# Stage seams of a two-layer decoder trunk: sums of squares on POOL, and weight splits queued behind the transposed input

## The chip, the cores and the metric

The kernel runs on one core of a Trainium2 chip. The metric is the device time of one execution in microseconds. The engines are named as the profile names them: PE (matrix products and transposes; PEld its weight loads), DVE (elementwise), ACT (activations and copies), POOL (a few small operations here), SP (issues loads). Each engine runs its instructions in the order in which they stand in its queue.

## What is computed

Two layers over 256 tokens of width 1024, in float32. Each layer is a SwiGLU FFN, a mixer, a second FFN, and a gated per-layer input embedding (PLE), each added to the running sum h and each behind an RMS norm:

```python
for i in range(DEPTH):
    h = h + 0.5 * swiglu(rmsnorm(h, ffn1_norm[i]), ffn1_wg[i], ffn1_wu[i], ffn1_wd[i])
    h = h + hybrid_mixer(rmsnorm(h, mix_norm[i]), w_in[i], ...)
    h = h + 0.5 * swiglu(rmsnorm(h, ffn2_norm[i]), ffn2_wg[i], ffn2_wu[i], ffn2_wd[i])
    gate = jax.nn.sigmoid(rmsnorm(h, ple_norm[i]) @ ple_w_gate[i])
    h = h + gate * (p[i] @ ple_w_proj[i])
return rmsnorm(h, final_norm)
```

`rmsnorm(h, g)` is `h * rsqrt(mean(h*h) + EPS) * g`, token by token. The mixer holds a gated short convolution and a Mamba-2 branch. The weights (some 270 MB) are read once.

## The kernel before

**Split products.** PE multiplies in a rounded format (fp32r). To keep float32 precision, each operand is split in two: a first part (the rounded value) and a second part (the rest), and three products are added. A weight chunk is loaded by SP in two halves of 128x1024 into `raw` tiles (`fetch`, lines 113 to 119; `NRAW` = 5 buffers). For each half ACT writes the first part `whi` (line 98) and DVE subtracts it from `raw` to get the second part `wlo` (line 96). A `raw` buffer is free, and its next load can be issued, when both have read it. There are seven pairs of `whi` and `wlo`.

**Order of the work.** The program is a list of items (`add`, line 133), each a function with the weight chunks that it reads. `emit` (lines 149 to 191) goes through the list; before each item `refill` splits as many coming halves as there are free pairs. The instructions thus recorded are then set in order for each engine by the compiler's scheduler, so that the queue of an engine can differ a little from the order of the code. `queued(ins)` (lines 106 to 111) orders the instructions of a block behind `ins` on its engine.

**A stage seam.** The tokens are two tiles of 128, tile 0 and tile 1. Between two stages stands a seam (`seam`, lines 353 to 370): the last products of the old stage, tile 0's first, then tile 1's; for each tile `finish` adds the result to h (line 538 for an FFN, line 1042 for the mixer), in two halves; `square` (line 326, ACT) gives for each half a sum of squares `ss`; `prepare` (lines 329 to 335) adds the two sums and EPS to `var` (line 288), takes the power -1/2 on POOL as `rstd` (line 294), and writes the normed tile `xn` on DVE (line 334). `turn` then transposes `xn` on PE (line 278, two groups of four), and splits the result into the first part of `xx` on ACT (line 281) and the second on DVE (line 282). The products of the new stage's head need `xx` of tile 0; PE does them while tile 1 is being normed, and turns tile 1 before the last step of the head for tile 0.

The held seams of the change are FFN to mixer, mixer to FFN, and FFN to PLE, each once in each layer. In the order of the text: the first seam is FFN to mixer, the second mixer to second FFN, the third FFN to PLE, and the fourth PLE to the next layer's FFN, which occurs once, since the second layer's PLE is followed by the final norm. In the third the products of the PLE projection (`between`, line 578) stand ahead of the head.

In each seam, halves of the coming stage's weights are split on DVE between the steps for tile 0 and tile 1.

Of the kernel before, what the change touches and what calls it, by code (L numbers as in the profile page):

```python
# [12 lines left out]
ALU = mybir.AluOpType  # L13
# [15 lines left out]
EPS = 1e-6  # L29
# [30 lines left out]
def trunk(ctx: ExitStack, tc: tile.TileContext, a: dict, out: bass.AP):  # L60
    nc = tc.nc
# [10 lines left out]
    def nm(s):  # L72
        cnt[0] += 1
        return f"{s}_{cnt[0]}"
# [19 lines left out]
    def split(hi, lo, src, later=None):  # L94
        def rest():
            return nc.vector.tensor_tensor(lo, src, hi.bitcast(F32), op=ALU.subtract).ins  # L96

        up = nc.scalar.activation(hi, src, AF.Copy).ins  # L98
        if later is None:
            rest()  # L100
        else:
            later.append(rest)
        return up

    @contextmanager
    def queued(*inss):

        with ExitStack() as order:
            for ins in inss:
                order.enter_context(tc.issue_after(ins))  # L110
            yield

    def fetch(src):
        raw = wp.tile([P, CH // 2], F32, tag="raw", name=nm("raw"), bufs=NRAW)
        if len(src.shape) == 2:
            nc.sync.dma_start(raw, src)
            return raw
        nc.sync.dma_start(raw.rearrange("p (j f) -> p j f", j=2), src)
        return raw.rearrange("p (j k c) -> p k j c", j=2, c=256)

    def half(raw, kn, later=None):

        hi = wp.tile([P, CH // 2], F32R, tag="whi", name=nm("whi"), bufs=NHALF)
        lo = wp.tile([P, CH // 2], F32R, tag="wlo", name=nm("wlo"), bufs=NHALF)
        up = split(*(w if len(raw.shape) == 2 else w.rearrange("p (k j c) -> p k j c", j=2, c=256) for w in (hi, lo)), raw, later)
        hv, lv = (w.rearrange("p (k c) -> p k c", k=kn) for w in (hi, lo))
        return [(hv[:, k], lv[:, k]) for k in range(kn)], up
# [2 lines left out]

    items, sources, loaded, ahead = [], {}, {}, []

    def add(fn, *keys):
        items.append((fn, keys))

    def chunk(name, i, c, kn):

# [10 lines left out]

    def emit():
        order, last = [], {}  # L150
        for n, (_, keys) in enumerate(items):
            for k in keys:
                if k not in last:
                    order += [(k, 0), (k, 1)]
                last[k] = n
        count = {"live": 0}
        raws = []
        coming = iter(order)
        waiting = iter(order)

        def load(most):
            while len(raws) < most:
                k, s = next(coming, (None, 0))
                if k is None:
                    return
                raws.append(fetch(sources[k][0][s]))

        def refill(most=NHALF, later=None):
            up = None
            while count["live"] < most:  # L170
                load(1)
                if not raws:
                    break
                k, s = next(waiting)
                wc, up = half(raws.pop(0), sources[k][1] // 2, later)
                loaded.setdefault(k, []).extend(wc)
                count["live"] += 1
            return up

        ahead.extend([load, refill])  # L180
        for n, (fn, keys) in enumerate(items):
            if n == 0:
                fn()
            else:
                refill()
                assert all(len(loaded[k]) == sources[k][1] for k in keys), keys
                fn(*[loaded[k] for k in keys])
            for k in set(keys):
                if last[k] == n:
                    count["live"] -= 2  # L190
                    del loaded[k]
# [93 lines left out]
    def rstd(parts, scale):  # L285
        v = sm.tile([P, 16], F32, tag="var", name=nm("var"))[:, 0:1]
        if len(parts) > 1:
            nc.vector.tensor_scalar(v, parts[0], parts[1], EPS, op0=ALU.add, op1=ALU.add)
            for p in parts[2:]:
                nc.vector.tensor_tensor(v, v, p, op=ALU.add)  # L290
        else:
            nc.vector.tensor_scalar(v, parts[0], scale, EPS, op0=ALU.mult, op1=ALU.add)
        r = sm.tile([P, 1], F32, tag="rstd", name=nm("rstd"))
        nc.gpsimd.tensor_tensor(r, v, mhalf, op=ALU.pow)  # L294
        return r

    class Norm:
# [31 lines left out]
        def prepare(self, t):  # L329
            r = rstd(self.ss[t], None)  # L330
            self.xn[t] = xn = act.tile([P, D], F32, tag="row", name=nm("xn"), bufs=2)
            for n, sl in enumerate(HALVES):
                g = self.g[n] if self.first else self.g[:, sl]
                ins = nc.vector.scalar_tensor_tensor(xn[:, sl], h[t][:, sl], r, g, op0=ALU.mult, op1=ALU.mult)  # L334
            self.ins[t] = ins.ins
# [3 lines left out]

    def closing(t, steps, finish, prep):

        def f(*wcs):
            for sl in prep.pieces[t]:
                for (fn, _), wc in zip(steps, wcs):
                    fn(wc, [sl])
                finish(t, sl)
                prep.square(t, sl)
            prep.prepare(t)  # L350
        add(f, *[k for _, keys in steps for k in keys])

    def seam(tail, finish, prep, between, head):
        for t in range(NT):
            steps, close = tail[t]
            if not head[0]:
                steps, close = (steps, close) if t == 0 else ([], steps + close)
            for fn, keys in steps:
                add(fn, *keys)
            if t == 1:  # L360
                add(lambda: prep.turn(0))
            closing(t, close, finish, prep)
        for fn, keys in between:
            add(fn, *keys)
        for n, (fn, keys) in enumerate(head[0]):
            if n == len(head[0]) - 1:
                add(lambda: prep.turn(1))
            add(fn, *keys)
        for fn, keys in head[1]:
            add(fn, *keys)  # L370
# [14 lines left out]
    class FFN:  # L385
# [151 lines left out]
        def finish(self, t, sl):  # L537
            nc.vector.scalar_tensor_tensor(h[t][:, sl], self.acc[t, sl.start], 0.5, h[t][:, sl], op0=ALU.mult, op1=ALU.add)  # L538
# [61 lines left out]
    class Mixer:  # L600
# [416 lines left out]
        def chain(self, g, c):  # L1017
            drip(len(fill))
            mp, i = self.pool, self.i
            if c == 0:  # L1020
                self.mn[g] = mp.tile([P, GW], F32, tag="mn", name=nm("mn"))
                nc.scalar.dma_start(self.mn[g], a["m_norm"][i:i + 1, g * GW:(g + 1) * GW].partition_broadcast(P))
            y = self.y[g, c]
            nc.vector.tensor_tensor(y, y, self.yps[g, c], op=ALU.add)
            nc.vector.tensor_tensor(y, y, self.sz[g, c], op=ALU.mult)
            junk = sm.tile([P, 512], BF16, tag="junk", name=nm("junk"), bufs=2)
            ss = sm.tile([P, 1], F32, tag="ss", name=nm("ss"))
            nc.scalar.activation(junk, y, AF.Square, accum_out=ss)
            self.rs[g, c] = rstd([ss], 1.0 / GW)
# [23 lines left out]
    class Last(Norm):  # L1053
# [12 lines left out]
        def prepare(self, t):  # L1066
            r = rstd(self.ss[t], None)
            xn = self.xn[t]
            nc.scalar.activation(xn[:, 0:512], xn[:, 0:512], AF.Copy, scale=r)
            nc.scalar.dma_start(out[t * P:(t + 1) * P, 0:512], xn[:, 0:512])  # L1070
            nc.vector.tensor_scalar(xn[:, 512:D], xn[:, 512:D], r, None, op0=ALU.mult)
            nc.sync.dma_start(out[t * P:(t + 1) * P, 512:D], xn[:, 512:D])
# [9 lines left out]
    prev = first  # L1082
    for s in stages[1:] + [None]:
        prep = s.prep if s else Last(a["final_norm"])
        add(prep.load)
        opening = [(prev.end, [])]
        if s:
            if not isinstance(s, Ple):
                opening.append((s.start, []))
            opening += getattr(s, "between", [])  # L1090
        seam(prev.tail, prev.finish, prep, opening, s.head if s else [[], []])
        if s:
            for fn, keys in s.body:
                add(fn, *keys)
            if isinstance(s, Mixer):
                add(s.load)
                seam(s.mo_tail, s.merge, s, [], s.wo.head)
        prev = s
    emit()


# [63 lines left out]
```

## Time and profile before

| what | value |
|---|---|
| median of 3 runs | 1525.07 us (1523.61 to 1526.6) |
| the profiled execution's own time | 1522.78 us |
| its span | 1520.4 us |
| busy, PE / DVE / ACT / POOL | 99% / 69% / 60% / 1% |
| granted PE clock | 0.999 |
| power on POOL (`rstd`), one | 0.55 us |
| split on DVE (`wlo`), one | 1.22 us |

A row of a timeline has the start from the span's beginning, the duration, the engine, the line, the operation, what is written and read (buffer numbers left out), the shape, the count (x4 is four in a row that are shown as one, their starts overlapping the ends a little), and in brackets the idle time before it and what ended that. A row of the waits has the total, the count and the longest.

### The profile page before, as it was taken

Reading aid. Unit: us, or ns where it says so; the run is one execution under the profiler, and the core shown is the slowest. Engines: PE = TensorE matmul, PEld = TensorE weight load, DVE = VectorE, ACT = ScalarE, POOL = GpSimd, SP = SyncE. Lnnn points to the kernel's source line nnn. Section 1 sums busy time; section 2 is a strip of 40 time slices with the busy share of each in tenths; the row PEclk is TensorE's granted clock in tenths of the full one; section 3 lists DMA queues with packets and bytes.
Section 4 is the critical chain, followed back from the end, with each engine's and each line's share of the span. In section 5 each row is a group of like instructions: output and inputs, shape, how many; then the busy total and the mean of one; then the engine's idle time right before and its main releaser. Section 6 shows DMA issues by size and latency. Waiting matters only on the chain.

```text
span 1520.4 us, 21065 instructions
## 1 busy us (share of the span) xinstructions
PE 1501.2 (99%) x7793; PEld 1273.1 (84%) x7793; DVE 1045.9 (69%) x1511; ACT 915.6 (60%) x1468; POOL 21.6 (1%) x41
## 2 busy tenths in 40 slices
PE   9999999999999999999999999999999999999997
PEld 6888888888888878888878888888888888888886
DVE  6766469898865567764677755588888655776545
ACT  6555368888754366553656544678887544655544
POOL 0000000000000000000000000000000000000000
PEclk9999999999999999999999999999999999999999
DMA  7665565656646556556565655655665565656642
GB/s 276 209 193 186 175 208 173 209 167 202 195 150 196 192 187 202 192 183 194 173 214 182 192 183 172 209 198 168 201 187 174 171 191 183 219 185 193 187 157 87
DMA packets 85432, 285.59 MB, mean 188 GB/s; under 512 B 10577, under 2 KB 10961, under 8 KB 85330
## 3 DMA queue, kind: packets, MB, share of 16 engines
q1 hardware_dynamic: 77968, 267.94, 54.3%
q10 hardware_dynamic: 7362, 16.31, 3.2%
q8 instruction: 61, 1.00, 0.3%
q14 instruction: 41, 0.34, 0.1%
HBM read 283.10 MB, written 1.11 MB: 187 GB/s over the span
## 4 chain that ended last, share of the span: by engine, by line
PE 89%; DVE 5%; ACT 2%; issue 2%; DMA 1%; POOL 1%; SPq 0%; POOLq 0%; ACTq 0%; DVEq 0%
PE ps L80 87%; DVE wlo L96 2%; PE ps L278 1%; DMA raw<-in_gu 1%; POOL rstd L294 1%; DVE xn L334 1%; DVE ac L862 0%; DMA m<-acD 0%; ACT whi L98 0%; PE ps L638 0%; ACT m L980 0%; DVE xx L282 0%; ACT L864 0%; PE ps L439 0%; ACT junk L326 0%
## 5 line engine op out<-in xcount | busy, mean ns | idle before, releaser
L96 DVE TENSOR_TENSOR wlo<-raw,whi 128x1024 fp32r<-128x1024 f32 x508 | 616.4, 1223 | 296.8 <-ACT whi L98 236.8
L98 ACT ACTIVATE whi<-raw 128x1024 fp32r<-128x1024 f32 x508 | 535.5, 1060 | 326.2 <-PE ps L80 291.6
L80 PE MATMUL ps<-xx,whi 128*128 128x512 f32 x1920 | 472.1, 394 | 0.0
L80 PEld LDWEIGHTS ps<-xx,whi 128*128 128x128 f32 x1920 | 350.8, 188 | 70.5 <-issue 4.3
L80 PE MATMUL ps<-whi,xx 128*128 128x512 f32 (+1 forms) x1168 | 369.4, 392 | 2.5 <-ACT whi L98 1.6
L80 PEld LDWEIGHTS ps<-whi,xx 128*128 128x128 f32 x1168 | 217.8, 188 | 48.7 <-ACT whi L98 3.2
L80 PEld LDWEIGHTS ps<-xx,wlo 128*128 128x128 f32 x1920 | 245.8, 191 | 8.9
L80 PE MATMUL ps<-xx,wlo 128*128 128x256 f32 x1920 | 249.6, 283 | 0.0
L80 PE MATMUL ps<-wlo,xx 128*128 128x512 f32 (+1 forms) x584 | 222.9, 388 | 0.8 <-DVE wlo L96 0.8
L80 PE MATMUL ps<-whi,hh 128*128 128x512 f32 x352 | 137.3, 390 | 0.0
L80 PE MATMUL ps<-wlo,hh 128*128 128x512 f32 x352 | 137.0, 389 | 0.0
L80 PEld LDWEIGHTS ps<-wlo,xx 128*128 128x128 f32 x584 | 109.9, 188 | 23.3 <-DVE wlo L96 2.3
L80 PE MATMUL ps<-whi,hl 128*128 128x512 f32 x352 | 113.6, 389 | 0.0
L394 ACT ACTIVATE sg<-ps 128x256 f32<-128x256 f32 x72 | 27.8, 386 | 111.5 <-PE ps L80 111.5
L80 PEld LDWEIGHTS ps<-whi,hl 128*128 128x128 f32 x352 | 66.1, 188 | 13.8
L80 PEld LDWEIGHTS ps<-whi,hh 128*128 128x128 f32 x352 | 66.1, 188 | 13.6
L80 PEld LDWEIGHTS ps<-wlo,hh 128*128 128x128 f32 x352 | 66.1, 188 | 13.6
L96 DVE TENSOR_TENSOR hl<-pr,hh 128x256 fp32r<-128x256 f32 x72 | 30.6, 425 | 58.3 <-ACT hh L98 58.3
L80 PE MATMUL ps<-whi,yh 128*128 128x512 f32 x128 | 50.0, 390 | 0.0
L80 PE MATMUL ps<-wlo,yh 128*128 128x512 f32 x128 | 49.8, 389 | 0.0
L326 ACT ACTIVATE junk<-h 128x512 bf16<-128x512 f32 (+1 forms) x37 | 22.6, 612 | 38.7 <-DVE h L538 28.4
L980 ACT ACTIVATE m<-m,acum 128x128 f32<-128x128 f32 x128 | 41.2, 391 | 4.9 <-DMA m<-acD 4.9
(162 smaller groups left out, 1176.1 us busy)
## 6 DMA issues: line engine op xcount, KB each, us to landing
raw<-in_gu SPq DMA_DIRECT2D x176, 512.0 KB, 3.8
raw<-in_dn SPq DMA_DIRECT2D x88, 512.0 KB, 3.6
raw<-in_w_xbc SPq DMA_DIRECT2D x48, 512.0 KB, 4.3
raw<-in_w_sc SPq DMA_DIRECT2D x48, 512.0 KB, 4.2
raw<-in_w_z SPq DMA_DIRECT2D x32, 512.0 KB, 4.1
raw<-in_w_mo SPq DMA_DIRECT2D x32, 512.0 KB, 3.8
raw<-in_w_ga SPq DMA_DIRECT2D x16, 512.0 KB, 4.5
m<-acD ACTq DMA_DIRECT2D x16, 512.0 KB, 4.9
```

Source lines behind the costliest of these rows:

```text
L80: return nc.tensor.matmul(o, lhsT=l, rhs=r, start=start, stop=stop).ins
L96: return nc.vector.tensor_tensor(lo, src, hi.bitcast(F32), op=ALU.subtract).ins
L98: up = nc.scalar.activation(hi, src, AF.Copy).ins
L278: nc.tensor.transpose(tp[:, j * P:(j + 1) * P], src[:, c:c + P], ident)
L294: nc.gpsimd.tensor_tensor(r, v, mhalf, op=ALU.pow)
L326: self.squared = nc.scalar.activation(junk[:, 0:sl.stop - sl.start], h[t][:, sl], AF.Square, scale=1.0 / 32.0, accum_out=ss).ins
L334: ins = nc.vector.scalar_tensor_tensor(xn[:, sl], h[t][:, sl], r, g, op0=ALU.mult, op1=ALU.mult)
L394: nc.scalar.activation(v, ps[:, 256:512], AF.Copy)
L980: nc.scalar.activation(m[:, hh], m[:, hh], AF.Relu, scale=-1.0, bias=self.acum[:, r0 + hh:r0 + hh + 1])
```

## The change

1. `rstd` adds the parts of a sum of squares (two, and a third for the last tile) on POOL instead of DVE, so that sum and power stand on one engine. A group norm with a single part stays on DVE.
2. `add` takes a `behind`. From tile 0's closing item in a held seam on, the second parts (`wlo`) of all halves that `refill` splits are not recorded, but kept in `held`. When the turn of tile 0 has been recorded, they are recorded too, ordered on DVE behind the second half of tile 0's `xx`. A held part whose chunk an item needs before that is recorded ahead of this item. The first parts on ACT stay where they were.
3. `seam` gets `hold`, true where the stage before isn't a PLE and a stage follows.

```diff
-    def add(fn, *keys):
-        items.append((fn, keys))
+    def add(fn, *keys, behind=None):
+        items.append((fn, keys, behind))
...
-                wc, up = half(raws.pop(0), sources[k][1] // 2, later)
+                rests = []
+                wc, up = half(raws.pop(0), sources[k][1] // 2, rests if held is not None else later)
+                if held is not None:
+                    held.extend((k, r) for r in rests)
...
+                if behind and held is None:
+                    held = []
                 refill()
...
+                if held:
+                    for k, r in held:
+                        if k in keys:
+                            r()
+                    held[:] = [kr for kr in held if kr[0] not in keys]
                 fn(*[loaded[k] for k in keys])
+                ins = behind and behind()
+                if held and ins:
+                    with queued(ins):
+                        for _, r in held:
+                            r()
+                if ins:
+                    held = None
...
-            nc.vector.tensor_scalar(v, parts[0], parts[1], EPS, op0=ALU.add, op1=ALU.add)
+            nc.gpsimd.tensor_scalar(v, parts[0], parts[1], EPS, op0=ALU.add, op1=ALU.add)
             for p in parts[2:]:
-                nc.vector.tensor_tensor(v, v, p, op=ALU.add)
+                nc.gpsimd.tensor_tensor(v, v, p, op=ALU.add)
...
-        add(f, *[k for _, keys in steps for k in keys])
+        add(f, *[k for _, keys in steps for k in keys], behind=(lambda: None) if hold else None)
...
-                add(lambda: prep.turn(0))
-            closing(t, close, finish, prep)
+                add(lambda: prep.turn(0), behind=(lambda: prep.turned[1]) if hold else None)
+            closing(t, close, finish, prep, hold and t == 0)
...
-        seam(prev.tail, prev.finish, prep, opening, s.head if s else [[], []])
+        seam(prev.tail, prev.finish, prep, opening, s.head if s else [[], []], hold=s is not None and not isinstance(prev, Ple))
```

Where it moves instructions on DVE. In the first layer's first seam (FFN to mixer) the queue before, from tile 0's sum of squares on; `h_84` is tile 1's running sum, `xn_1789` and `xn_1878` are the normed tiles 0 and 1:

```order
L288 TENSOR_SCALAR var_1785<-ss_1761,ss_1783 128x1
L334 SCALAR_TENSOR_TENSOR xn_1789<-h_83,rstd_1787,gain_1738 128x512 x2
L96 TENSOR_TENSOR wlo_1807<-raw_1804,whi_1806 128x1024
L96 TENSOR_TENSOR wlo_1813<-raw_1810,whi_1812 128x1024
L96 TENSOR_TENSOR wlo_1831<-raw_1828,whi_1830 128x1024
L96 TENSOR_TENSOR wlo_1837<-raw_1834,whi_1836 128x1024
L282 TENSOR_TENSOR xx_1740<-ps_1840,xx_1740 128x4x128
L282 TENSOR_TENSOR xx_1740<-ps_1847,xx_1740 128x4x128
L538 SCALAR_TENSOR_TENSOR h_84<-ps_1448,h_84 128x512
L538 SCALAR_TENSOR_TENSOR h_84<-ps_1449,h_84 128x512
```

The same place after (line numbers of the changed file, 20 or 21 higher behind the edit):

```order
L354 SCALAR_TENSOR_TENSOR xn_1789<-h_83,rstd_1787,gain_1738 128x512 x2
L302 TENSOR_TENSOR xx_1740<-ps_1836,xx_1740 128x4x128
L302 TENSOR_TENSOR xx_1740<-ps_1843,xx_1740 128x4x128
L96 TENSOR_TENSOR wlo_1807<-raw_1804,whi_1806 128x1024
L96 TENSOR_TENSOR wlo_1812<-raw_1809,whi_1811 128x1024
L96 TENSOR_TENSOR wlo_1829<-raw_1826,whi_1828 128x1024
L96 TENSOR_TENSOR wlo_1834<-raw_1831,whi_1833 128x1024
L559 SCALAR_TENSOR_TENSOR h_84<-ps_1448,h_84 128x512
L559 SCALAR_TENSOR_TENSOR h_84<-ps_1449,h_84 128x512
L96 TENSOR_TENSOR wlo_1884<-raw_1881,whi_1883 128x1024
L96 TENSOR_TENSOR wlo_1890<-raw_1887,whi_1889 128x1024
L354 SCALAR_TENSOR_TENSOR xn_1878<-h_84,rstd_1876,gain_1738 128x512 x2
```

The four splits have moved from ahead of tile 0's `xx` to behind it, still ahead of tile 1's `h`; the sum `var` has left the queue. The third seam moves alike.

In the second seam (mixer to FFN) of the first layer the queue after, from tile 0's `h` on; before, the split of `raw_5047` (here `wlo_5049`) stood ahead of the first row, and the other four behind `xn`:

```order
L1063 TENSOR_TENSOR h_83<-h_83,ps_4972 128x512
L1063 TENSOR_TENSOR h_83<-h_83,ps_4973 128x512
L354 SCALAR_TENSOR_TENSOR xn_5076<-h_83,rstd_5074,gain_5024 128x512 x2
L302 TENSOR_TENSOR xx_5026<-ps_5123,xx_5026 128x4x128
L302 TENSOR_TENSOR xx_5026<-ps_5130,xx_5026 128x4x128
L96 TENSOR_TENSOR wlo_5049<-raw_5046,whi_5048 128x1024
L96 TENSOR_TENSOR wlo_5094<-raw_5091,whi_5093 128x1024
L96 TENSOR_TENSOR wlo_5099<-raw_5096,whi_5098 128x1024
L96 TENSOR_TENSOR wlo_5116<-raw_5113,whi_5115 128x1024
L96 TENSOR_TENSOR wlo_5121<-raw_5118,whi_5120 128x1024
L1063 TENSOR_TENSOR h_84<-h_84,ps_5027 128x512
```

Five splits now stand behind `xx`, one of them the first that the head's products read. In the fourth seam, where nothing is held, one of the two splits that stood between tile 1's `h` and its `xn` has moved behind `xn`. PE's and SP's orders stay as they were, but for a few rows of PE in the second and fourth seams.

More of the change, by code (lines that the diff above doesn't have):

```diff
@@ L150, in emit @@
         order, last = [], {}
-        for n, (_, keys) in enumerate(items):
+        for n, (_, keys, _) in enumerate(items):
             for k in keys:
@@ L178, in refill @@
             return up
+        held = None
         ahead.extend([load, refill])
-        for n, (fn, keys) in enumerate(items):
+        for n, (fn, keys, behind) in enumerate(items):
             if n == 0:
@@ L184, in emit @@
             else:
+                if behind and held is None:
+                    held = []
                 refill()
                 assert all(len(loaded[k]) == sources[k][1] for k in keys), keys
-                fn(*[loaded[k] for k in keys])
+                if held:
[3 more added lines that the diff above has]
+                    held[:] = [kr for kr in held if kr[0] not in keys]
+                fn(*[loaded[k] for k in keys])
+                ins = behind and behind()
[4 more added lines that the diff above has]
+                if ins:
+                    held = None
             for k in set(keys):
@@ L338, in turn, with closing @@
             self.turned = flip(self.xn[t], self.x[0], self.x[1], t)
-    def closing(t, steps, finish, prep):
+    def closing(t, steps, finish, prep, hold):
         def f(*wcs):
@@ L350, in f, with seam @@
             prep.prepare(t)
-        add(f, *[k for _, keys in steps for k in keys])
-    def seam(tail, finish, prep, between, head):
+        add(f, *[k for _, keys in steps for k in keys], behind=(lambda: None) if hold else None)
+    def seam(tail, finish, prep, between, head, hold=False):
         for t in range(NT):
```

## Prediction

> **What bounds the kernel now.** I read the page first, then the waits of PE, then the timeline of each engine at the seams between stages.
>
> ```profile
> PE 1501.2 (99%) x7793; PEld 1273.1 (84%) x7793; DVE 1045.9 (69%) x1511; ACT 915.6 (60%) x1468; POOL 21.6 (1%) x41
> ...
> PE ps L278 <- DVE xn L334: 2.4, 5, 1.4
> ...
> PE ps L80 <- DVE wlo L96: 0.8, 2, 0.5
> PE ps L80 <- DVE xx L282: 0.6, 1, 0.6
> ```
>
> PE is busy 99% of the span, so nothing can be gained but the rest, and every microsecond that PE is made to wait is added to the time. In the waits of PE (total, times, longest) all seams together cost 2.4 us at the transposes of a normed tile, 0.8 us for a second part and 0.6 us for a transposed input. The gain that the change can reach is small; what it can lose has no such limit. So I look at what stands on DVE between the two tiles of a seam. DVE and ACT at the first FFN-to-mixer seam (start, us, instruction):
>
> ```profile
> 190.31 1.41 DVE L334 SCALAR_TENSOR_TENSOR xn<-h,rstd,gain 128x512 f32<-128x512 f32 x2 [0.66 <-POOL rstd L294]
> 191.64 4.63 DVE L96 TENSOR_TENSOR wlo<-raw,whi 128x1024 fp32r<-128x1024 f32 x4
> 196.19 1.28 DVE L282 TENSOR_TENSOR xx<-ps,xx 128x512 fp32r<-128x512 f32 x2
> 197.38 1.28 DVE L538 SCALAR_TENSOR_TENSOR h<-ps,h 128x512 f32<-128x512 f32 x2
> 198.58 2.35 DVE L96 TENSOR_TENSOR wlo<-raw,whi 128x1024 fp32r<-128x1024 f32 x2
> 200.85 0.21 DVE L288 TENSOR_SCALAR var<-ss,ss 128x1 f32<-128x1 f32 x1
> 201.72 1.41 DVE L334 SCALAR_TENSOR_TENSOR xn<-h,rstd,gain 128x512 f32<-128x512 f32 x2 [0.66 <-POOL rstd L294]
> ...
> 189.36 1.06 ACT L98 ACTIVATE whi<-raw 128x1024 fp32r<-128x1024 f32 x1
> ...
> 194.42 1.07 ACT L281 ACTIVATE xx<-ps 128x512 fp32r<-128x512 f32 x2
> ...
> 198.29 0.61 ACT L326 ACTIVATE junk<-h 128x512 bf16<-128x512 f32 x1
> ...
> 199.43 0.19 ACT L326 ACTIVATION_READ_ACCUMULATOR junk<-h 128x1 f32 x1
> ```
>
> From tile 0's xn to tile 1's xn DVE works without a break but for the 0.66 us in which POOL takes the power. The four splits from 191.64 fill just the time in which tile 0 is being turned on PE and copied by ACT (until 195.49). Tile 1's xn is the next thing that PE needs, and it is already late by a little:
>
> ```profile
> 193.20 1.03 PE L278 MATMUL ps<-ident,xn 128*128 128x128 f32 x8
> ...
> 202.02 0.39 PE L80 MATMUL ps<-whi,xx 128*128 128x512 f32 x1
> 202.62 0.63 PE L278 MATMUL ps<-ident,xn 128*128 128x128 f32 x4 [0.20 <-DVE xn L334]
> ...
> 543.15 1.03 PE L278 MATMUL ps<-ident,xn 128*128 128x128 f32 x8
> ...
> 546.99 0.39 PE L80 MATMUL ps<-wlo,xx 128*128 128x512 f32 x1
> ...
> 552.63 0.63 PE L278 MATMUL ps<-ident,xn 128*128 128x128 f32 x4 [0.27 <-DVE xn L334]
> ...
> 728.27 1.03 PE L278 MATMUL ps<-ident,xn 128*128 128x128 f32 x8
> ...
> 742.76 1.03 PE L278 MATMUL ps<-ident,xn 128*128 128x128 f32 x8
> ```
>
> Tile 0's turns (193.20, 543.15, 728.27) wait for nothing. Tile 1's turns wait in the first two seams (FFN to mixer, mixer to FFN), not in the third (FFN to PLE). So tile 1's xn is what ends last, and DVE's queue ahead of it decides.
>
> **The change part by part.** *The held splits.* The order after puts them behind tile 0's xx and ahead of tile 1's residual sum h. DVE then stands idle while tile 0 is turned (nothing else of its queue can pass), and does the splits where it used to prepare tile 1. Step by step, first seam: ACT's two copies end at 195.49. How long DVE needs after them shows in the second seam, where DVE waits for nothing else:
>
> ```profile
> 544.37 1.07 ACT L281 ACTIVATE xx<-ps 128x512 fp32r<-128x512 f32 x2
> ...
> 555.12 1.08 ACT L281 ACTIVATE xx<-ps 128x512 fp32r<-128x512 f32 x2
> ...
> 555.75 1.29 DVE L282 TENSOR_TENSOR xx<-ps,xx 128x512 fp32r<-128x512 f32 x2
> ...
> 541.66 4.62 DVE L96 TENSOR_TENSOR wlo<-raw,whi 128x1024 fp32r<-128x1024 f32 x4
> ...
> 551.73 1.42 DVE L334 SCALAR_TENSOR_TENSOR xn<-h,rstd,gain 128x512 f32<-128x512 f32 x2 [0.66 <-POOL rstd L294]
> ```
>
> ACT ends at 556.20, DVE at 557.04: 0.84 us later. So the first seam's xx is ready at 196.33; starts overlap ends by 0.09, so the four splits run from 196.25 to 200.8 (4.55 from start to next start), h to 202.0 (1.20), the two further splits to 204.3 (2.27). Tile 1's xn cannot start before 204.3 instead of 201.72: +2.6 by DVE alone, the var of 0.21 and the handoff already taken away.
>
> A second chain is longer. The raw buffers are five, and SP's next load waits for the split that frees one:
>
> ```profile
> 192.89 1.59 SPq L116 DMA_DIRECT2D raw<-in_w_ga  x2
> ...
> raw<-in_w_ga SPq DMA_DIRECT2D x2, 512.0 KB, 4.4
> ...
> raw<-in_gu SPq DMA_DIRECT2D x8, 512.0 KB, 4.8
> ```
>
> The load at 192.89 follows the end of the first split (191.64 + 1.22). It brings the raw of the second of the "two further splits", whose first part on ACT stands ahead of tile 1's squares, before and after. Held, the first split ends at 197.5, the load lands 4.4 us later at 201.9 (medians of the two seams' own windows, last column, in us), ACT's first part takes 1.06 (to 203.0), the two squares 1.33 (198.29 to 199.62, so to 204.3), the sum on POOL 0.4, the power 0.55 (below), 205.3. From xn's start to the turn go 0.90 us (201.72 to 202.62). Turn at 206.2 instead of 202.62: **+3.6 us, twice**.
>
> Second seam: five splits are held, since one of them stood ahead of tile 0's own h. xx is ready at 545.44 + 0.84 = 546.28. The head's second product, due at 546.99, needs the first held split, done at 547.4: a new wait of 0.45 us, part of what follows. The load that matters follows the second held split (548.55), lands 4.8 us later at 553.4, first part 554.45, squares 555.8, sum and power 556.75, turn 557.7 instead of 552.63: **+5.1 us, twice**. By DVE alone (five splits at 1.14, h 1.20, two splits 2.27) xn could start at 555.4 instead of 551.73: +3.6.
>
> Third seam: as in the first, four splits, and the same 13.0 us from turn to turn (193.20 to 206.2) would give 741.3. PE comes there at 742.76, because the PLE projection lies between. **0**, with 1.5 us to spare; without that cover it would cost as the first.
>
> *The sums on POOL.*
>
> ```profile
> 1.08 0.29 POOL masks.py:199 TENSOR_SCALAR_AFFINE_SELECT ident<-ident 128x128 f32<-128x128 f32 x1
> ...
> 189.73 0.55 POOL L294 TENSOR_TENSOR rstd<-var,mhalf 128x1 f32<-128x1 f32 x1 [176.06 <-DVE var L288]
> ...
> 767.01 1.40 POOL L294 TENSOR_TENSOR rstd<-var,mhalf 128x1 f32<-128x1 f32 x1 [8.72 <-DVE var L288]
> ...
> 765.53 1.22 DVE L96 TENSOR_TENSOR wlo<-raw,whi 128x1024 fp32r<-128x1024 f32 x1
> 766.66 0.20 DVE L288 TENSOR_SCALAR var<-ss,ss 128x1 f32<-128x1 f32 x1
> 766.79 1.21 DVE L96 TENSOR_TENSOR wlo<-raw,whi 128x1024 fp32r<-128x1024 f32 x1
> 768.44 1.41 DVE L334 SCALAR_TENSOR_TENSOR xn<-h,rstd,gain 128x512 f32<-128x512 f32 x2 [0.44 <-POOL rstd L294]
> ...
> 1515.07 0.16 DVE L290 TENSOR_TENSOR var<-var,ss 128x1 f32<-128x1 f32 x1 [0.18 <-ACT junk L326]
> 1515.38 0.55 POOL L294 TENSOR_TENSOR rstd<-var,mhalf 128x1 f32<-128x1 f32 x1 [6.46 <-DVE var L290]
> ```
>
> No sum on POOL stands in the trace. Its power on one element a partition takes 0.55, a select on 128 takes 0.29; I take 0.4, between. Where DVE was free, the sum was 0.3 us on the way (1515.07 to 1515.38), so tile 0's norms and the last one change by 0.1 each; tile 0's are hidden by products, **the last is +0.1** (bounds 0 to +0.3). Where DVE was not free, the move is worth more: in the fourth seam (PLE to FFN, where nothing is held) the order after has one split ahead of tile 1's xn instead of two. Sum after the split (766.75) by 767.15, power 767.7, turn 0.90 later at 768.65, instead of 768.44 + 0.90 = 769.34: **-0.7**, once.
>
> But the same rows show a price: the power of 767.01 took 1.40, and ended 0.41 after the split at 766.79 had (768.00). POOL waited for DVE's operation with two inputs. The Trainium skill ("SBUF — State Buffer", section "SBUF: two separate sides") says that such an operation and one of POOL lock each other out for the whole instruction; this row agrees, and the rule speaks against moving work to POOL. In the held seams the sum can meet the last split before xn: up to 0.41 more at each of four turns, 1.6 in all; I leave it out of the sum and in the range.
>
> Sum: 2 x 3.6 + 2 x 5.1 + 0 - 0.7 + 0.1 = +16.8. The profiled execution took 1522.78 (span 1520.4 and 2.4 around it), so 1539.6; the median of the runs, 1525.07, is 2.3 above it, so I forecast **1541.9**.
>
> **The rivals.** *DVE alone.* If loads land soon enough, only the queue counts: 2 x 2.6 + 2 x 3.6 - 0.7 + 0.1 = +11.8, 1536.9. For it: the load goes into empty queues and may be quicker than a median over loads that queue. Against: the chain is 0.9 to 1.5 us longer in the medians. Chance 0.2.
>
> *POOL locked out.* The four sums and powers meet splits, +1.6, and 1543.5. For it the row of 767.01; against, most powers stand at 0.55. By the rule above every sum that meets a split would pay. Chance 0.12.
>
> *The hold is hidden (other side).* Tile 1's chain would be early: its waits at the turns (the rows' idle of 0.20 and 0.27, twice each) vanish as var leaves DVE, and with -0.7 and +0.1 that is -1.5: 1523.6. It decides where tile 1's xn starts by 201.5 (202.62 less the 0.20 and the 0.90); held splits would have to be done by 197.4, when h can start, and they start at 196.25. If PE came to tile 1 five us later, as in the third seam (14.5 from turn to turn instead of 9.4), it would be so everywhere. Chance 0.07; the same time follows if the hold did not act, but the order shows that it does (0.03).
>
> *Late loads.* ACT issues the mixer's constants at the same time; landings a microsecond and more later give +1 at each of four turns, the third seam starts to pay, 1546 to 1548. Chance 0.08.
>
> **How the numbers follow.** The forecast has 0.5. Range: from 1534 (below DVE alone, with quicker turns) to 1548 (late loads and lockout); outside are the hidden hold and little more. A difference under 0.2%, 3 us, is about what a measurement of this kernel can tell from no change. Faster 0.03 (the hidden hold with a further microsecond), same 0.07, slower 0.90.
>
> **What would show it.** Right: DVE idle for some 3 us between tile 0's xn and xx; PE's wait for xn at tile 1's turns 3 to 5 us, four times, and none in the third seam; a wait of about 0.45 for wlo at the head of the second seam; SP's loads 4.6 us later in the first seam; one turn earlier in the fourth seam. Wrong: tile 1's turns without a wait, or a wait ended by POOL and not by DVE's queue; then the hold was hidden, or the lock is the cause.

## The result, and the profile after

The kernel after takes 1543.82 us (median of 4 runs, 1543.04 to 1544.21), the kernel before 1524.34 us beside it (4 runs, 1521.72 to 1526.6). The ratio is 1.0126, with a 95% interval of 1.011 to 1.0143. The profiled execution after took 1543.6 us (span 1541.9), 20.8 us more than the one before.

The page's first lines of the kernel after:

```profile
PE 1508.3 (98%) x7793; PEld 1278.9 (83%) x7793; DVE 1043.5 (68%) x1492; ACT 916.9 (59%) x1468; POOL 31.1 (2%) x60
```

Its waits of PE (total, times, longest):

```profile
PE ps L298 <- DVE xn L354: 18.3, 6, 5.8
...
PE ps L80 <- DVE wlo L96: 1.1, 3, 0.5
```

The waits for `xn` at the turns have gone from 2.4 to 18.3 us. That is 15.9 of the 21.5 us of span. Another 7.1 us stand in PE's busy time: 1508.3 for the same 7793 products that took 1501.2 before. The rest of PE's idle time is 1.5 us less.

DVE and ACT at the first seam of the first layer, kernel after:

```profile
190.14 1.41 DVE L354 SCALAR_TENSOR_TENSOR xn<-h,rstd,gain 128x512 f32<-128x512 f32 x2 [1.84 <-POOL rstd L314]
194.68 1.29 DVE L302 TENSOR_TENSOR xx<-ps,xx 128x512 fp32r<-128x512 f32 x2 [3.13 <-ACT xx L301]
195.89 4.62 DVE L96 TENSOR_TENSOR wlo<-raw,whi 128x1024 fp32r<-128x1024 f32 x4
200.43 1.28 DVE L559 SCALAR_TENSOR_TENSOR h<-ps,h 128x512 f32<-128x512 f32 x2
201.63 2.35 DVE L96 TENSOR_TENSOR wlo<-raw,whi 128x1024 fp32r<-128x1024 f32 x2
204.82 1.42 DVE L354 SCALAR_TENSOR_TENSOR xn<-h,rstd,gain 128x512 f32<-128x512 f32 x2 [0.85 <-POOL rstd L314]
...
201.19 1.06 ACT L98 ACTIVATE whi<-raw 128x1024 fp32r<-128x1024 f32 x1 [4.09 <-DMA raw<-in_w_ga]
202.16 0.61 ACT L346 ACTIVATE junk<-h 128x512 bf16<-128x512 f32 x1
...
197.17 1.47 SPq L116 DMA_DIRECT2D raw<-in_w_ga  x2
...
203.57 0.57 POOL L308 TENSOR_SCALAR var<-ss,ss 128x1 f32<-128x1 f32 x1 [13.47 <-ACT junk L346]
204.23 0.56 POOL L314 TENSOR_TENSOR rstd<-var,mhalf 128x1 f32<-128x1 f32 x1
```

DVE stands idle for 3.13 us while tile 0 is turned, and the four splits run behind `xx`. The load that went out at 192.89 before goes out at 197.17 now; ACT waits 4.09 us for it, and tile 1's squares stand behind that first part. Tile 1's `xn` then waits 0.85 us for the power, not for the splits ahead of it: the last of them ends at 203.98.

PE at the turns of tile 1 in the first and second seams of both layers, kernel after (four pieces; the rows behind a turn are the next products):

```profile
205.72 1.69 PE L298 MATMUL ps<-ident,xn 128*128 128x128 f32 x8 [3.66 <-DVE xn L354]
207.06 0.78 PE L80 MATMUL ps<-whi,xx 128*128 128x512 f32 x1
207.63 0.63 PE L80 MATMUL ps<-wlo,xx 128*128 128x512 f32 x1
208.06 1.05 PE L80 MATMUL ps<-whi,xx 128*128 128x512 f32 x2
208.91 0.63 PE L80 MATMUL ps<-wlo,xx 128*128 128x512 f32 x1
...
550.92 0.50 PE L80 MATMUL ps<-wlo,xx 128*128 128x512 f32 x1 [0.30 <-DVE wlo L96]
...
560.62 1.69 PE L298 MATMUL ps<-ident,xn 128*128 128x128 f32 x8 [4.17 <-DVE xn L354]
...
1324.20 1.94 PE L298 MATMUL ps<-ident,xn 128*128 128x128 f32 x8 [5.84 <-DVE xn L354]
```

The eight transposes take 1.64 to 1.94 us, where those of tile 0 before took 1.03, and the products behind them start 0.43 us apart (207.63, 208.06, then 0.85 for two) where 0.23 is usual. The windows of 3.6 us from each of the four turns on (start and end, length, PE's busy time and count, granted clock):

```profile
205.72:209.30 3.58, 3.58 (x13) 0.56 1.02 418
560.60:564.20 3.60, 3.58 (x13) 0.57 0.99 396
966.60:970.20 3.60, 3.57 (x13) 0.60 0.99 372
1324.20:1327.80 3.60, 3.60 (x13) 0.50 0.63 233
```

The same stretch before:

```profile
202.60:206.20 3.60, 3.58 (x19) 1.00 0.53 187
```

So PE not only waits, it also runs at about half its clock for some microseconds after the wait. The Trainium skill ("TensorE: Matmul & The Clock Gate", section "Part 1: The HAM clock gate (the "warmup" mystery)") says that PE's clock falls to half after an idle window of some 3.4 us, and that the window runs freely. These four waits, 3.66 to 5.84 us, agree with that; shorter ones in other runs do not fit it (last section).

How much later PE starts an instruction than in the kernel before, from the starts of the same instruction by its position in PE's order (all in us):

| seam | ahead of the turn | at tile 1's turn | some ten products on | wait, predicted | slow clock |
|---|---|---|---|---|---|
| first, layer 1 | -0.33 | 3.10 | 4.51 | +3.43 (3.6) | +1.41 |
| second, layer 1 | 3.47 | 7.99 | 9.53 | +4.52 (5.1) | +1.54 |
| third, layer 1 | 9.53 | 9.53 | 9.53 | 0 (0) | 0 |
| fourth | 9.53 | 8.80 | 8.80 | -0.73 (-0.7) | 0 |
| first, layer 2 | 8.80 | 12.13 | 13.68 | +3.33 (3.6) | +1.55 |
| second, layer 2 | 13.33 | 19.52 | 21.66 | +6.19 (5.1) | +2.14 |
| third, layer 2, and PE's last product | 21.68 | 21.68 | 21.69 | 0 (0) | 0 |

In the second seams "ahead of the turn" is ahead of tile 0's, so their waits hold the one at the head, 0.46 and 0.47. The last norm stands behind PE's last product and does not show here; ACT waits 1.01 us for its power, 0.92 before: the predicted +0.1. Between the seams 0.33, 1.04 and 0.35 are won back (start, layer 1's mixer, layer 2's mixer).

### The profile page after: what moved, and what is told of

Same layout as the page of the kernel before. It is cut to its first block, busy times and chain, and to the rows that moved or that the text cites. A ratio compares the mean times of both kernels' runs of the same rounds, so it can differ in the third digit from the quotient of the medians.

```text
span 1541.9 us, 21067 instructions
## 1 busy us (share of the span) xinstructions
PE 1508.3 (98%) x7793; PEld 1278.9 (83%) x7793; DVE 1043.5 (68%) x1492; ACT 916.9 (59%) x1468; POOL 31.1 (2%) x60
## 4 chain that ended last, share of the span: by engine, by line
PE 67%; issue 26%; DVE 3%; ACT 2%; DMA 1%; POOL 1%; POOLq 0%; ACTq 0%; DVEq 0%; SPq 0%
PE ps L80 65%; DVE wlo L96 1%; PE ps L298 1%; POOL rstd L314 1%; ACT whi L98 0%; DMA m<-acD 0%; ACT junk L346 0%; PE ps L659 0%; DVE ac L883 0%; POOL var L308 0%; DMA raw<-in_gu 0%; DVE xx L302 0%; DMA out<-xn 0%; DVE y L1046 0%; ACT m L1001 0%
## 5 line engine op out<-in xcount | busy, mean ns | idle before, releaser
L302 DVE TENSOR_TENSOR xx<-ps,xx 128x512 fp32r<-128x512 f32 x40 | 25.9, 686 | 31.6 <-ACT xx L301 31.2
```

Of the source, the lines that this page charges most:

```text
L302: down = nc.vector.tensor_tensor(lo[:, ks, t], v, hi.bitcast(F32)[:, ks, t], op=ALU.subtract)
```

## The experiments

All ratios are to the kernel before, on the same chip, with their 95% intervals. The theory: the held splits delay tile 1's loads, and with them ACT's first part, squares, `xn` and turn. The first rival is DVE's queue alone, the second POOL, locked out by DVE's splits.

**One part alone.** The sums on POOL with nothing held (`hold=False` in the last call of `seam`):

```diff
-        seam(..., hold=s is not None and not isinstance(prev, Ple))
+        seam(..., hold=False)
```

> Only the sums on POOL, nothing held. Theory (the cost is the hold): 1.0 to 2.5 us below the kernel before: about -1 from the fourth seam, and at most -0.9 from the waits of 0.20 and 0.27 at tile 1's four turns in the first two seams. POOL locked out: every sum that meets a split pays up to 0.41, seven turns, so +1 to +3.

Measured: 1523.41 against 1523.47 us, 1.0004 (0.9992 to 1.0015). The cost of the change is not in the sums, but the expected gain didn't come either. DVE's splits and tile 1's sum in the second seam of layer 1, the sum in that of layer 2, and DVE and POOL in the first seam, sums alone:

```profile
549.31 2.35 DVE L96 TENSOR_TENSOR wlo<-raw,whi 128x1024 fp32r<-128x1024 f32 x2
...
550.32 1.51 POOL L308 TENSOR_SCALAR var<-ss,ss 128x1 f32<-128x1 f32 x1 [9.31 <-ACT junk L346]
...
1301.30 1.51 POOL L308 TENSOR_SCALAR var<-ss,ss 128x1 f32<-128x1 f32 x1 [9.31 <-ACT junk L346]
...
199.11 2.35 DVE L96 TENSOR_TENSOR wlo<-raw,whi 128x1024 fp32r<-128x1024 f32 x2
202.31 1.41 DVE L354 SCALAR_TENSOR_TENSOR xn<-h,rstd,gain 128x512 f32<-128x512 f32 x2 [0.85 <-POOL rstd L314]
...
200.49 1.14 POOL L308 TENSOR_SCALAR var<-ss,ss 128x1 f32<-128x1 f32 x1 [9.68 <-ACT junk L346]
201.71 0.56 POOL L314 TENSOR_TENSOR rstd<-var,mhalf 128x1 f32<-128x1 f32 x1
```

A sum that takes 0.30 us alone takes up to 1.51 beside splits. The one at 200.49 starts while the second split runs and ends at 201.63, 0.17 after it. The one at 550.32 starts while the first of the two splits runs and ends at 551.83, 0.17 after the second: POOL was not let in between the two. PE's idle at tile 1's turns is 0.38 and 0.47 instead of 0.20 and 0.27 in layer 1, 0.42 and 0.47 instead of 0.32 and 0.24 in layer 2, which eats what the fourth seam gives.

The hold alone (lines 308 and 310 back to `nc.vector`):

```diff
-            nc.gpsimd.tensor_scalar(v, parts[0], parts[1], EPS, op0=ALU.add, op1=ALU.add)
+            nc.vector.tensor_scalar(v, parts[0], parts[1], EPS, op0=ALU.add, op1=ALU.add)
...
```

> Only the hold, sums on DVE as before. Theory: as the kernel after or 0.5 to 1.5 above it (the fourth seam's gain is gone), so 19.5 to 21 above the kernel before. POOL locked out: the sums on POOL cost something in the held seams, so this one is 1 to 3 below the kernel after.

Measured: 1547.74 against 1523.47 us, 1.016 (1.0142 to 1.0177); its profiled execution took 1544.03, that of the kernel after 1543.6. The whole cost is the hold, and it is not less without the sums on POOL: PE's idle at the four turns is 4.12, 4.79, 4.16 and 4.90. By the medians this kernel is 24 us above the one before, more than the 19.5 to 21 expected; its five runs lie at 1544 and at 1548 to 1549, and why was not tried. POOL's lock as the cause of the slowdown falls.

**Two held of four.** The first two held, the rest ahead of `xx` as before:

```diff
+                    for n_, (k, r) in enumerate(held):
+                        if k in keys or n_ >= 2:
                             r()
...
```

> After, but only the first two second parts of each held seam are held, the others stay ahead of xx. Theory (late loads set tile 1's turn): the buffers that these two free are those of the loads that tile 1's squares stand behind, so the turns stay within 0.5 us of the kernel after, and the time 15 to 20 above the kernel before. DVE's queue alone: 2.27 less ahead of tile 1's h in the first seam and 3.4 less in the second, so all but 0 to 1 per turn of the cost is gone, 0 to 4 above the kernel before.

Or only the last two (the first two of a seam, three in the second, aren't kept):

```diff
-                wc, up = half(..., rests if held is not None else later)
+                wc, up = half(..., rests if held is not None and not skip else later)
...
```

> After, but only the last two second parts of each held seam are held. Theory (late loads): the loads go out as before, DVE's queue then allows tile 1's xn 0.3 later in the first seam and 0 to 0.3 later in the second, so -1 to +1.5 against the kernel before. DVE's queue alone: the same as with the first two held, 0 to 4 above the kernel before; what tells the theories apart is the difference of the two kernels, 15 or more against none.

Measured: 1529.9 and 1527.29 against 1523.47 us, 1.0039 (1.0024 to 1.0054) and 1.0026 (1.0015 to 1.0038). The difference of 15 that the theory named is not there, and by the letter of the expectation it falls. But the pair did not do what it was made for. The loads of the first seam, the first kernel's and then the second's:

```profile
194.10 1.70 SPq L116 DMA_DIRECT2D raw<-in_w_ga  x2
```

```profile
193.19 1.53 SPq L116 DMA_DIRECT2D raw<-in_w_ga  x2
```

Both went out early, at the end of the first split that each kernel has ahead of `xx` (it started at 192.85 and 191.95): in these two traces, as in those of the kernels before and after, the load follows whichever split stands first in DVE's queue, not that of the first half. So both kernels have early loads, and the pair only shows that two held cost 4 to 6 us and four or five some 20. What is left of the cost in them is in part POOL's: in the first seam tile 1's sum takes 1.40 us in both, and `xn` waits 0.76 for the power.

**The two further halves.** Between DVE's queue and the load's chain the following kernels decide. First only DVE's second parts of the two further halves go behind tile 1's `xn` (`pend` is `xn`'s second half):

```diff
-                refill()
+                with queued(*pend):
+                    refill()
+                pend = ()
...
```

> After, but the two further second parts of tile 1's step are queued on DVE behind tile 1's xn; ACT's first parts stay ahead of tile 1's squares. Theory (late loads set the turn through ACT's queue): xn waits for the power, not for DVE (the splits were done at 203.97, the power at 204.79), so 0 to 1 us below the kernel after. DVE's queue alone: 2.27 at each of four turns, so 9 below it.

Measured: 1544.7 against 1523.96 us, 1.0142 (1.0123 to 1.016), the same as the kernel after within the intervals. DVE and ACT in the first seam of this kernel:

```profile
200.82 1.28 DVE L565 SCALAR_TENSOR_TENSOR h<-ps,h 128x512 f32<-128x512 f32 x2
205.18 1.42 DVE L358 SCALAR_TENSOR_TENSOR xn<-h,rstd,gain 128x512 f32<-128x512 f32 x2 [3.08 <-POOL rstd L318]
...
201.83 1.06 ACT L98 ACTIVATE whi<-raw 128x1024 fp32r<-128x1024 f32 x1 [4.34 <-DMA raw<-in_w_ga]
202.79 0.61 ACT L350 ACTIVATE junk<-h 128x512 bf16<-128x512 f32 x1
```

DVE, rid of the two splits, waits 3.08 us for the power; PE's idle at the turn is 3.62 instead of 3.66. The two splits between tile 1's `h` and its `xn` do not set the turn.

Then ACT's first parts go behind tile 1's squares too (`pend` holds the second square as well):

```diff
-            f.late = lambda: (prep.ins[t],)
+            f.late = lambda: (prep.squared, prep.ins[t])
```

> As the run before, but ACT's first parts of the same two halves stand behind tile 1's squares too. Theory: tile 1's squares follow h at 201.7, turn at 204.5 instead of 205.7 in the first seam (1.2 each) with a wait short enough that fewer slow products follow (up to 1.4 each); in the second seam 1 to 3 each: 5 to 10 below the kernel after in all. DVE's queue alone: no difference from the run before.

Measured: 1551.6 against 1523.96 us, 1.0181 (1.0162 to 1.0201), slower. Not a test of the theory after all: the order on ACT closed up, and other work came ahead of the squares. ACT in the first seam:

```profile
201.48 1.28 ACT L941 ACT_TABLE_LOAD   x1 [6.31 <-DMA raw<-in_w_ga]
204.66 0.23 ACT L941 ACTIVATE negA<-alog 128x32 f32<-128x32 f32 x1 [1.90 <-DMA alog<-in_A_log]
204.80 0.61 ACT L350 ACTIVATE junk<-h 128x512 bf16<-128x512 f32 x1
```

The squares now stood behind a table load (L941) and behind a small constant, for whose landing ACT waited 1.90 us. So everything was put behind them that ACT has to do there:

```diff
-                fn(*[loaded[k] for k in keys])
+                with queued(*pend):
+                    fn(*[loaded[k] for k in keys])
...
```

> As late_refill, but everything else that ACT does between tile 1's residual sum and its turn (the constants' loads, the table load, the first activations of the next stage) stands behind tile 1's squares as well. Theory (the late loads set the turn through ACT's queue): the squares follow h at 201.7, sum and power end at 203.5, turn at 204.4 instead of 205.7 in the first seam, 1.5 to 3 sooner in the second: 5 to 9 us below the kernel after. If the turn comes at 205.7 all the same, something else than the load sets it.

Measured: 1535.99 against 1524.78 us, 1.0072 (1.0052 to 1.0091), 8 us less than the kernel after by the ratios. ACT, POOL, DVE and PE in the first seam:

```profile
201.96 0.63 ACT L352 ACTIVATE junk<-h 128x512 bf16<-128x512 f32 x1 [6.09 <-DVE h L569]
...
203.39 0.30 POOL L314 TENSOR_SCALAR var<-ss,ss 128x1 f32<-128x1 f32 x1 [12.56 <-ACT junk L352]
...
204.37 1.42 DVE L360 SCALAR_TENSOR_TENSOR xn<-h,rstd,gain 128x512 f32<-128x512 f32 x2 [1.93 <-POOL rstd L320]
...
205.27 1.23 PE L304 MATMUL ps<-ident,xn 128*128 128x128 f32 x8 [2.48 <-DVE xn L360]
```

Now the squares wait for `h`, so for DVE's queue, and PE's idle is 2.48 instead of 3.66 (2.98 instead of 4.17 and 5.84 in the second seam). Of the 1.2 us in the first seam, 0.9 is ACT's (the squares start 0.80 after `h` does, 1.73 in the kernel after) and 0.3 POOL's (the sum takes 0.30 instead of 0.57). The late load is what ended last in the kernel after; behind it stands DVE's queue ahead of `h`, the held splits themselves, worth 2.5 to 3 us at each turn. So more than half of each wait would be there without the late load.

**The clock.** 24 transposes of the identity ahead of tile 1's turn in the first and second seams:

```diff
+            for _ in range(fillers if b == 0 else 0):
+                nc.tensor.transpose(tp[:, 0:P], ident, ident)
...
```

> After, with 24 transposes of the identity, about 2.7 us, on PE ahead of tile 1's turn in the first and second seams, into a bank that the turn overwrites. Theory (products run at half the clock because PE was idle): the products behind the turn stand 0.227 apart instead of 0.427, so 4 to 7 us below the kernel after. Rival (they are slow because of their operands or of traffic of the other engines): no change, within 1 us of the kernel after.

Measured: 1541.8 against 1523.96 us, 1.0121 (1.0104 to 1.0138); the span is 1539.4, in the kernel after 1541.9, so 2.5 us less where 4 to 7 were expected. PE in the first and second seams with 24 fillers:

```profile
202.07 2.78 PE L297 MATMUL ps<-ident 128*128 128x128 f32 x24
205.79 1.32 PE L300 MATMUL ps<-ident,xn 128*128 128x128 f32 x8 [0.93 <-DVE xn L356]
...
560.94 1.78 PE L300 MATMUL ps<-ident,xn 128*128 128x128 f32 x8 [2.11 <-DVE xn L356]
```

The windows behind these two turns (the granted clock is the third figure from the right):

```profile
205.79:209.50 3.71, 3.71 (x20) 1.00 1.01 402
560.90:565.00 4.10, 4.06 (x15) 0.58 0.87 297
```

The turn of the first seam comes at the same time as in the kernel after (205.79 against 205.72), but the products behind it run at full clock: the slow clock there is the idle. In the second seam 2.11 us of idle were left and it stayed slow. With more fillers there:

```diff
-        seam(..., fillers=24 if s is not None and not isinstance(prev, Ple) and not isinstance(s, Ple) else 0)
+        seam(..., fillers=24 if isinstance(s, Mixer) else 36 if isinstance(prev, Mixer) else 0)
```

> As fill24, with 36 transposes of the identity in the second seam, so that less than 2 us of idle is left there. Theory (half clock after some 2 us of idle): the products behind the second seam's turns stand 0.227 apart as well, 1.0 to 1.5 each, so 2 to 3 us below fill24 and 4 to 6 below the kernel after. Rival: no change against fill24.

Measured: 1540.79 against 1524.78 us, 1.0111 (1.0092 to 1.0129). The clock followed the theory. PE at the second seam's turn, and then the same window as above, with more fillers:

```profile
562.17 1.32 PE L300 MATMUL ps<-ident,xn 128*128 128x128 f32 x8 [0.83 <-DVE xn L356]
```

```profile
560.90:565.00 4.10, 3.27 (x21) 1.00 0.98 377
```

The time did not: the span is 1539.3 against 1539.4, since the turn itself came 1.2 us later (562.17 against 560.94). Put side by side by position in PE's order, the two traces show that these 1.2 us arose ahead of the seam: 0.6 in the first 14 us, 0.5 at about 317 in the mixer, where PE waited 0.62 instead of 0.16 us for `xw`, and the rest ahead of tile 0's turn. Behind the turns the products win 1.4 us in each layer, which is the slow clock's price there; layer 2's first seam and mixer take as much away again in longer waits. Why PE waited longer in these places was not tried.

**What is better than both.** The order that the experiments point to is the opposite one: nothing held, and in the seams that the change holds tile 1's squares and `xn` ahead of the two further halves, with the sums on POOL (`closing` gets a flag `late`):

```diff
+        if late:
+            f.late = lambda: (prep.squared, prep.ins[t])
...
-                add(lambda: prep.turn(0), behind=(lambda: prep.turned[1]) if hold else None)
+                add(lambda: prep.turn(0), behind=None)
...
```

> Sums on POOL, nothing held, and in the seams that the change holds tile 1's squares and xn stand ahead of the two further halves on ACT and DVE. Theory (tile 1's chain is what ends last at a seam): the waits for xn at tile 1's turns go, 1 to 3 us below the kernel before and 0 to 1.5 below the sums alone. Rival (the two halves are then late themselves): a new wait for a second part in the head, 0 to 2 above the sums alone.

Measured: 1519.2 against 1523.96 us, 0.9972 (0.9959 to 0.9984), by the medians 4.8 us less, more than the 1 to 3 expected. POOL and PE in the first seam of this kernel, then its row of PE's waits at the turns:

```profile
199.93 0.30 POOL L312 TENSOR_SCALAR var<-ss,ss 128x1 f32<-128x1 f32 x1 [9.33 <-ACT junk L350]
...
202.44 1.03 PE L302 MATMUL ps<-ident,xn 128*128 128x128 f32 x8
```

```profile
PE ps L302 <- DVE xn L358: 0.9, 2, 0.5
```

With no split beside it the sum takes 0.30, and the turn waits for nothing. The same with the sums on DVE:

```diff
-            nc.gpsimd.tensor_scalar(v, parts[0], parts[1], EPS, op0=ALU.add, op1=ALU.add)
+            nc.vector.tensor_scalar(v, parts[0], parts[1], EPS, op0=ALU.add, op1=ALU.add)
...
```

> As late_nohold, but the sums on DVE as before: only tile 1's squares and xn ahead of the two further halves. Theory (the order gives the gain, and POOL's sum costs the same once no split stands beside it): within 0.5 us of late_nohold in the first and second seams, about 1 more for the fourth seam, so 3 to 4.5 below the kernel before. Rival (the sums on POOL give the gain): no gain, within 1 us of the kernel before.

Measured: 1521.71 against 1524.78 us, 0.9981 (0.997 to 0.9992). The order gives a gain by itself; its only idle of any size at a turn is 1.40 us in the fourth seam. And the same order in the fourth seam too:

```diff
-            closing(t, close, finish, prep, False, hold and t == 1)
+            closing(t, close, finish, prep, False, t == 1 and type(prep) is Norm)
```

> As late_nohold, with tile 1's squares and xn ahead of the two further halves in the fourth seam too. Theory: the idle of 0.54 that is left there at tile 1's turn goes, 0 to 0.6 below late_nohold, 4 to 6 below the kernel before.

Measured: 1520.37 against 1524.78 us, 0.9967 (0.9958 to 0.9977). It is faster than the kernel before and the kernel after; against the version without the fourth seam the intervals overlap, and the idle of 0.54 there became 0.49 only.

## Why the prediction was right, and where not

**Right: what ends last at a seam, and its price.** The prediction put the four waits at 2 x 3.6 + 2 x 5.1 = 17.4 us; they come to 3.43 + 4.52 + 3.33 + 6.19 = 17.5. The chain it named is the one that the runs show: a turn that doesn't move when DVE's splits are taken out of `xn`'s way, and a wait that is 1.2 us shorter at three turns, and 2.9 at the fourth, when ACT's late first part is. *DVE alone* was wrong by that much, though DVE's queue ahead of `h` makes more than half of each wait; the rival of the hidden hold and that of POOL were wrong too.

One sign of being wrong came by its letter: POOL's power, and not DVE's queue, ended `xn`'s wait (0.85 us). It does not mean what the prediction said, the lock. The squares themselves were late, as the predicted chain has it, and the hold alone costs as much with the sums on DVE.

**Right by compensation: the second seam.** The median of 4.8 us for the load was taken for both layers. In layer 1 the turn came sooner than said, in layer 2 later. ACT's wait for the second of the two further loads, kernel after, layer 1 and layer 2:

```profile
556.35 1.06 ACT L98 ACTIVATE whi<-raw 128x1024 fp32r<-128x1024 f32 x1 [0.62 <-DMA raw<-in_gu]
...
1319.95 1.06 ACT L98 ACTIVATE whi<-raw 128x1024 fp32r<-128x1024 f32 x1 [2.24 <-DMA raw<-in_gu]
```

The difference in the two waits, 1.6 us, is the difference of the two turns (6.19 less 4.52). Which traffic made the second load slow was not tried. This is a part of what the rival *late loads* said, at one turn of four.

**Right: the third seam, the head of the second, the fourth seam.** No wait in the third; 0.46 and 0.47 for the second part at the head, said 0.45; -0.73 in the fourth, said -0.7. The sum on POOL was taken at 0.4; alone it takes 0.30.

**Missing: the slow clock after the wait.** The sum priced a wait at its length. After each of the four long waits PE ran some ten instructions at half clock: 1.41 + 1.54 + 1.55 + 2.14 = 6.6 us that the prediction has no term for. That is the step that failed: "every microsecond that PE is made to wait is added to the time" is a lower bound where the wait is long. Against it stand 1.7 us won back between the seams (0.33 + 1.04 + 0.35), and 0.7 around the span (1.7 instead of 2.4). So the profiled execution took 1543.6 instead of 1539.6. The median of the kernel after lies only 0.2 above its profiled execution; the 2.3 that the prediction added for the median hid half of the gap, by luck.

**POOL's lock: too small for the sum, within the bound at the turn.** It was bounded by 0.41 at each turn, from a row with one split. Without the hold a sum takes up to 1.2 longer (1.51 less 0.30), since POOL waits for two splits in a row. PE's idle at the turns grows by 0.10 to 0.23 only, since before the sum stood behind these splits too, in DVE's queue. In the kernel after it costs little, since tile 1's sum comes when the splits are nearly or wholly done (0.57 at 203.57).

## What to carry to other kernels

Ask of every split, copy or load that is moved which buffer it frees, and follow the freed buffer to the next load and to whatever stands behind that load in another engine's queue: here that chain ended 0.9 us and more behind the queue of the moved instructions. Put the work that the bottleneck engine needs next ahead of work that only fills time, on each engine that it passes; here this order was worth 0.3% where the change cost 1.3%. Price a wait of PE of 3.5 us and more at its length and 1.1 to 2.3 us on top: so much longer than before took the stretch from the start of tile 1's turn to the ninth product behind it after each of 16 waits of 3.48 to 7.69 us (in the kernel after, the hold alone, and the first two kernels of *The two further halves*). The price does not follow the length; behind the longest wait it was 1.13. Later waits can take back a part of it, as the kernel after shows between its seams.

## What was not expected of the hardware

- In the kernel after the granted clock was 0.50 to 0.60 in the 3.6 us behind each idle of 3.66 to 5.84 us. Below that it was not a matter of the length alone: behind the turns after 0.83, 0.93 and 2.48 us no product was slow, after 2.98 us some were in one layer and none in the other, and after 2.11 us some were, right behind 21 of the 24 fillers (three had run earlier). The Trainium skill ("TensorE: Matmul & The Clock Gate", section "Part 1: The HAM clock gate (the "warmup" mystery)") gives an idle window of some 3.4 us; slow products after 2.98 and 2.11 us differ from that figure, so it is no lower bound here. No run shows the window itself. The fillers count as work, at least in part: with 24 and 36 of them ahead of the turn PE did no product for 3.7 and 4.6 us, of which under 1 us was idle, and the clock stayed at 1.00.
- A sum of one element a partition on POOL takes 0.30 us alone. Beside a split of DVE it ends 0.17 after that split (1.14 for the one at 200.49, sums alone). Five sums of that kernel started near the end of the first of two splits in a row and took 1.48 to 1.51: they ended behind the second, so POOL got no turn between the two. It is not so for every pair: a power that started at 338.69, beside another product of DVE with a split right behind it, took 0.86 and ended while that split ran (339.07 to 340.29).
